# Cross-covariance attention on one core: stores two units later, and outputs of ten units laid out four heads wide

## The chip, the cores and the metric

The kernel runs on one core of a Trainium2 chip. The metric is the device time of one launch in microseconds (us). Engines are named as in the profile: PE is the matrix engine (PEld its weight loads), DVE the vector engine, ACT the scalar engine, POOL GpSimd, SP the engine whose queue issues every transfer here.

## The reference

```python
# Q, K, V: (8, 12, 512, 64) float32
Q_norm = Q / (np.linalg.norm(Q, axis=-2, keepdims=True) + 1e-10)
K_norm = K / (np.linalg.norm(K, axis=-2, keepdims=True) + 1e-10)
attn = np.einsum('bhnd,bhne->bhde', Q_norm, K_norm)          # 64 x 64 per head
attn = softmax(attn, axis=-1)
return np.einsum('bhnd,bhde->bhne', V, attn)                 # 512 x 64 per head
```

There are 96 heads. Three inputs and one output of 12.58 MB each have to cross between HBM and the core, 50.33 MB in all.

## The kernel before

**Units and pairs.** Four heads make a unit, so there are 24 units (u = 0 to 23). Q and K of a unit come as one 512 KB transfer each (`load_qk`, L72 and L73): partition 32h + i holds 16 successive rows of head h, 4 KB in one run. V comes for two units at once, a pair w = 0 to 11, as one 1 MB transfer (`load_v`, L77): each partition holds 32 successive rows, 8 KB in one run. The output of a unit goes out as one 512 KB transfer (`store`, L80), that of the last unit as two of 256 KB.

**One unit's way.** DVE casts Q and K to bfloat16, side by side (`cast_q` L84, `cast_k` L87). PE forms the Gram matrix of the joined 128 columns of each head (`grams`, 64 matmuls, L103): its diagonal gives both norms (`norms`, L115, L120), one off-diagonal block gives the logits. ACT saves that block (`keep_kq`), POOL scales it, PE transposes it (`logits`), DVE scales and ACT takes exponentials (`exps`, L139). `normalise` (L143 to L147) writes the softmax in bfloat16 into one of 12 buffers `ab`; `doubled` (L176, L177) copies it through PE and ACT to the other 64 partitions, so that `ab` holds a block diagonal of two copies and one matmul serves two rows of V.

**V and the outputs.** V of a pair is cast by ACT and DVE (`cast_v`, L96), transposed on PE eight 128x128 blocks at a time (`vtrans`, L155), and evicted by ACT into `vt` (L159). In `outs` (L179) the transposed V is the weight and `ab` the moving operand. An output bank `po` holds 128 partitions x 512 numbers: for two heads, x = 0 and 1, 64 columns of weights each (`MV = 64`), and four steps t. So a unit takes two banks of eight matmuls, each partition of a bank holds eight successive rows, and `store` writes runs of 2 KB:

```python
Of = out.rearrange("b h n d -> (b h n d)").rearrange("(u s p f) -> u p s f", s=SV, p=128, f=TP * 2 * D)
```

With A = 4 and TP = 4 a partition's 16 pieces of V are numbered (a, t).

**The order.** The program order of each engine is written out by hand. A main loop runs over steps s = 0 to 23: loads for unit s + 3, V loads, stores of the units up to `n1 - 3`, where `outs_by(s) = (s - 3) * 9 // 10` is the number of units whose outputs are computed by the end of step s; then the Gram part of unit s, logits of s - 1, normalisation of s - 2, outputs, and transposes of V. After step 23 a second loop computes the outputs of units 18 to 23 (i = 0 to 5): the Gram banks of PSUM are given over to a pool `ps_t` of four banks, in which `vtrans_f32` (L170, L171) transposes the last V uncast; `outs` there evicts one bank by ACT and one by DVE; `doubled(last)` stands at i = 3, ahead of the outputs of unit 21. The outputs use the two banks of `ps_o` throughout.

**Queues.** SP issues all 85 transfers in program order. Eight completion semaphores are handed out in turn, so each transfer waits until the one eight places before it has landed, and besides for its data or its buffer: a load of Q and K for the cast five units back (five buffers), a V load for the cast five pairs back, a store for its unit's evictions. An eviction of `outs` waits until the store ten units back has landed (ten buffers `so`).

Of the kernel before, what the change touches and what calls it, by code (L numbers as in the profile page):

```python
# [8 lines left out]
F32 = mybir.dt.float32  # L9
BF16 = mybir.dt.bfloat16  # L10
# [4 lines left out]
D = 64  # L15
HU = 4
# [1 line left out]
R = 16  # L18
HV = 8
NP = 16  # L20
A = 4
SV = 2
MV = 64
TP = 4


@with_exitstack
def kernel(
# [7 lines left out]
    nc = tc.nc  # L36
    B, H, N, _ = Q.shape
    assert N == NV * R and Q.shape[3] == D
    U = B * H // HU

    Qf, Kf = (x.rearrange("b h n d -> (b h n d)").rearrange("(u p f) -> u p f", p=128, f=R * D) for x in (Q, K))
    Vf = V.rearrange("b h n d -> (b h n d)").rearrange("(w p f) -> w p f", p=128, f=2 * R * D)
    Of = out.rearrange("b h n d -> (b h n d)").rearrange("(u s p f) -> u p s f", s=SV, p=128, f=TP * 2 * D)

    ctx.enter_context(tc.manual_schedule())

# [3 lines left out]
    vbp = ctx.enter_context(tc.tile_pool(name="vbp", bufs=3))  # L50
    qkp = ctx.enter_context(tc.tile_pool(name="qkp", bufs=4))
    vtp = ctx.enter_context(tc.tile_pool(name="vtp", bufs=3))
# [3 lines left out]
    ps_v = ctx.enter_context(tc.tile_pool(name="ps_v", bufs=1, space=bass.MemoryType.PSUM))  # L56
    ps_l = ctx.enter_context(tc.tile_pool(name="ps_l", bufs=1, space=bass.MemoryType.PSUM))
    ps_o = ctx.enter_context(tc.tile_pool(name="ps_o", bufs=2, space=bass.MemoryType.PSUM))
# [3 lines left out]
    def outs_by(s):  # L62

        return max(0, (s - 3) * 9 // 10)


    qf, kf, vf, vb, qkb, nsq, rq, kqs, sl, ex, vt, so, kq = ({} for _ in range(13))
# [7 lines left out]
    def load_v(w):  # L75
        vf[w] = vp.tile([128, 2 * R * D], F32, name="vf")
        nc.sync.dma_start(out=vf[w], in_=Vf[w])  # L77

    def store(u, g=slice(0, SV)):
        nc.sync.dma_start(out=Of[u][:, g], in_=so[u][:, g].rearrange("p s t d -> p s (t d)"))  # L80

    def cast_q(u):
        qkb[u] = qkp.tile([128, R, 2 * D], BF16, name="qkb")
# [5 lines left out]
    def cast_v(v):  # L89

        w, i = divmod(v, 2)
        if i == 0:
            vb[w] = vbp.tile([128, A, TP, 2 * D], BF16, name="vb")
        x = vf[w].rearrange("p (a t d) -> p a t d", a=A, d=2 * D)
        for t, copy in ((2 * i, nc.scalar.copy), (2 * i + 1, nc.vector.tensor_copy)):
            copy(vb[w][:, :, t], x[:, :, t])  # L96

    def grams(u):

# [29 lines left out]
    def logits(u):  # L129
        for h in range(HU):  # L130
            nc.tensor.transpose(lg[:, h, :], kqs[u][D:, h, :], ident[D:, D:])  # L131

    def scale_q(u):
        s = sl[u] = small.tile([D, HU, D], F32, name="sl")
        nc.vector.tensor_tensor(out=s, in0=lg, in1=rq[u][0:D, :, None].to_broadcast([D, HU, D]), op=ALU.mult)  # L135

    def exps(u):
        e = ex[u] = small.tile([D, HU, D], F32, name="ex")
        nc.scalar.activation(e, sl[u], AF.Exp)  # L139

    def normalise(u):
        s = small.tile([D, HU], F32, name="esum")
        nc.vector.reduce_sum(out=s, in_=ex[u], axis=AX.X)  # L143
        ri = small.tile([D, HU], F32, name="rinv")
        nc.vector.reciprocal(ri, s)
        a = abuf[u % len(abuf)]
        nc.vector.tensor_tensor(out=a[0:D, :, 0, :], in0=ex[u], in1=ri[:, :, None].to_broadcast([D, HU, D]), op=ALU.mult)  # L147

    def vtrans(v):

        w, i = divmod(v, 2)
        ps = ps_v.tile([128, A, 2, 128], BF16, name="vps")
        for t in range(2):
            for a in range(A):
                nc.tensor.transpose(ps[:, a, t, :], vb[w][:, a, 2 * i + t, :], identb)  # L155

        if i == 0:
            vt[w] = vtp.tile([128, TP, 128, A], BF16, name="vt")
        nc.scalar.copy(vt[w][:, 2 * i:2 * i + 2], ps.rearrange("p a t c -> p t c a"))  # L159

    def vtrans_f32(v):

        w, i = divmod(v, 2)
        if i == 0:
            vt[w] = vtp.tile([128, TP, 128, A], BF16, name="vt")
        for t in range(2 * i, 2 * i + 2):
            ps = ps_t.tile([128, 128, A], F32, name="vps32")
            for a in range(A):
                c = (a * TP + t) * 2 * D
                nc.tensor.transpose(ps[:, :, a], vf[w][:, c:c + 2 * D], ident)  # L170
            both[t % 2](vt[w][:, t], ps)  # L171

    def doubled(u):

        a = abuf[u % len(abuf)]
        nc.tensor.matmul(dup[D:], identb[0:D, 0:D], a[0:D, :, 0, :], tile_position=(0, D))  # L176
        nc.scalar.copy(a[D:, :, 1, :], dup[D:])  # L177

    def outs(u, copies=(nc.scalar.copy, nc.scalar.copy)):  # L179
        s = so[u] = sop.tile([128, SV, TP, 2 * D], F32, name="so")  # L180
        a = abuf[u % len(abuf)]
        v = vt[u // 2][:, :, u % 2 * 64:(u % 2 + 1) * 64]
        for g in range(SV):
            po = ps_o.tile([128, TP, 2 * D], F32, name="po")
            for t in range(TP):
                for x in range(2):
                    h = 2 * g + x
                    nc.tensor.matmul(  # L188
                        po[MV * x:MV * (x + 1), t, :], v[:, t, NP * h:NP * (h + 1), :].rearrange("p c a -> p (c a)"),
                        a[:, h].rearrange("p a d -> p (a d)"), tile_position=(0, MV * x),  # L190
                    )
            copies[g](s[:, g], po)  # L192

# [10 lines left out]
    ident = const.tile([128, 128], F32, name="ident")  # L204
    make_identity(nc, ident)
    identb = const.tile([128, 128], BF16, name="identb")
# [7 lines left out]
    def clear(i):  # L214

        nc.scalar.copy(abuf[i].rearrange("p h a d -> p (h a d)"), zeros)
# [4 lines left out]
    def on(f, u):  # L221
        if 0 <= u < U:
            f(u)
# [3 lines left out]
    nv, nst, nt = 0, 0, 0  # L227
    for s in range(U):
        n0, n1 = outs_by(s - 1), outs_by(s)
        on(load_qk, s + LOAD_AHEAD)  # L230
        while nv < (min(U, n1 + 7) // 2 if s >= 3 else 1):
            load_v(nv)
            nv += 1
        while nst < n1 - 3:
            store(nst)
            nst += 1
        new = range(nt, max(0, min(s - 2, n1 + 2)))
        if s > 4:
            for v in new:
                cast_v(v)  # L240
        on(cast_q, s + 1)
        on(normalise, s - 2)
        on(grams, s)
        on(norms, s)
        on(keep_kq, s)
        on(scale_k, s)
        on(logits, s - 1)
        on(scale_q, s - 1)
        on(exps, s - 1)
        on(cast_k, s + 1)  # L250
        if s <= 4:
            for v in new:
                cast_v(v)
        for v in range(n0, n1):
            outs(v)
        on(doubled, s - 2)
        if 6 <= s + 5 < len(abuf):
            clear(s + 5)
        for v in new:
            vtrans(v)  # L260
            nt = v + 1

    last = U - 1
    main.close()
    ps_t = ctx.enter_context(tc.tile_pool(name="ps_t", bufs=4, space=bass.MemoryType.PSUM))
    both = (nc.scalar.copy, nc.vector.tensor_copy)

    for i, u in enumerate(range(n1, U)):
        while nv < min(U, u + 8) // 2:
            load_v(nv)  # L270
            nv += 1
        store(u - 3)
        if i == 0:
            normalise(last - 1)
        if i == 2:
            scale_q(last)
            exps(last)
        if i == 3:
            normalise(last)
        on(vtrans_f32, u + 2)  # L280
        if i == 1:
            doubled(last - 1)
        if i == 3:
            doubled(last)
        outs(u, both)
        if i == 1:
            logits(last)
    for u in range(U - 3, last):
        store(u)
    for g in range(SV):  # L290
        store(last, slice(g, g + 1))
# [29 lines left out]
```

## Time and profile before

| | |
|---|---|
| median of 11 runs | 131.05 us (130.54 to 131.91) |
| profiled execution | 131.2 us, span 129.4 us |
| busy | PE 86.1, PEld 66.3, DVE 95.1, ACT 91.2, POOL 64.7 us |
| transfers | 15208 packets, 50.67 MB, mean 392 GB/s |
| Q, K, V and store issues | 24, 24, 12 and 25 |

The span runs from the first to the last of the program's own instructions; what lies around it makes up the other 1.8 us. The share of a transfer queue is the time its packets took, as a share of 16 transfer engines over the whole span. A line of the timeline gives start, duration, engine, line and operation, then in brackets how long the engine had been idle and what ended that. A matmul group's duration holds the latency of its last matmul.

### The profile page before, as it was taken

To read this page: it belongs to the slowest core of one execution; us is meant where nothing else is said; L and a number is where in the kernel's file an instruction comes from. 1 tells how busy PE (TensorE), PEld (TensorE's weight loads), DVE (VectorE), ACT (ScalarE), POOL (GpSimd) and SP (SyncE) were. 2 spreads that over 40 slices of the span, in tenths; PEclk is the share of its full clock that TensorE was granted. 3 is DMA by queue.
4 is the path that set the end of the run, shared out by engine and by line. 5 is a ranking of instruction groups with operands and counts; after the bars stand their busy time and mean duration, and the time that the engine had idled before them with its cause. 6 is when DMAs were issued, how large, how long until landed. Compare 5 with 4: busy or idle time off the path is not lost.

```text
span 129.4 us, 5390 instructions
## 1 busy us (share of the span) xinstructions
PE 86.1 (67%) x2232; PEld 66.3 (51%) x2232; DVE 95.1 (73%) x366; ACT 91.2 (70%) x171; POOL 64.7 (50%) x57
## 2 busy tenths in 40 slices
PE   0047565958856976849883697688486497859530
PEld 0046543837644854638652576465364385648420
DVE  0445979596998699894994968987993889648740
ACT  7601353675999999899596565999699398997520
POOL 4006775672698168656564761986267077500000
PEclk9999999999998599995999658999999859999955
DMA  4999999999999999999999999999999999999894
GB/s 139 348 386 427 414 408 410 423 408 406 418 405 420 403 409 419 411 404 432 399 412 419 411 411 413 429 406 408 422 411 406 421 419 405 403 389 362 321 340 163
DMA packets 15208, 50.67 MB, mean 392 GB/s; under 512 B 1360, under 2 KB 1360, under 8 KB 13648
## 3 DMA queue, kind: packets, MB, share of 16 engines
q1 hardware_dynamic: 15184, 50.34, 97.6%
q8 instruction: 17, 0.28, 0.9%
q14 instruction: 7, 0.06, 0.1%
HBM read 37.75 MB, written 12.58 MB: 389 GB/s over the span
## 4 chain that ended last, share of the span: by engine, by line
DMA 45%; DVE 15%; ACT 15%; PE 13%; issue 4%; SPq 3%; ACTq 0%; DVEq 0%
DMA qf<-in_Q_dram 28%; DMA out_dram<-so 9%; DMA vf<-in_V_dram 8%; PE gram L103 5%; DVE scr L115 5%; ACT so L192 4%; ACT vt L159 3%; PE po L188 3%; PE vps L155 3%; ACT ex L139 2%; DVE qkb L84 2%; ACT kq L108 2%; ACT vb L96 2%; PE vps L170 2%; DVE ab L147 1%
## 5 line engine op out<-in xcount | busy, mean ns | idle before, releaser
L120 POOL TENSOR_TENSOR rq<-nsq,mhalf 128x4 f32<-128x4 f32 x24 | 47.8, 1992 | 45.2 <-DVE nsq L115 28.9
L103 PE MATMUL gram<-qkb 32*128 32x128 bf16 x1536 | 35.8, 256 | 16.3 <-DVE qkb L87 10.6
L103 PEld LDWEIGHTS <-qkb 32*128 32x128 bf16 x1536 | 29.8, 115 | 22.6 <-DVE qkb L87 13.3
L115 DVE CUSTOM_DVE_ANT_0 scr<-gram,ident 128x128 f32<-128x128 f32 x96 | 22.0, 281 | 9.5 <-PE gram L103 9.5
L108 ACT COPY kq<-gram 64x256 f32<-64x256 f32 x24 | 8.8, 368 | 26.4 <-DVE nsq L115 26.2
L84 DVE CAST qkb<-qf 128x1024 bf16<-128x1024 f32 x24 | 16.6, 690 | 12.3 <-DMA qf<-in_Q_dram 12.3
L192 ACT COPY so<-po 128x512 f32<-128x512 f32 x42 | 22.8, 588 | 2.0 <-PE po L188 1.5
L188 PE MATMUL po<-ab,vt 128*64 128x128 bf16 x384 | 18.2, 232 | 5.4 <-ACT vt L159 2.9
L159 ACT COPY vt<-vps 128x1024 bf16<-128x1024 bf16 x20 | 20.2, 1012 | 0.7
L188 PEld LDWEIGHTS <-vt 128*64 128x64 bf16 x384 | 12.6, 115 | 9.6 <-ACT vt L159 4.1
L155 PEld LDWEIGHTS <-vb 128*128 128x128 bf16 x160 | 10.9, 110 | 12.8 <-ACT kq L108 6.3
L87 DVE CAST qkb<-kf 128x1024 bf16<-128x1024 f32 x24 | 16.2, 675 | 0.5 <-DMA kf<-in_K_dram 0.5
L125 POOL TENSOR_TENSOR kqs<-kq,rq 64x256 f32<-64x256 f32 x24 | 15.4, 641 | 1.9
L155 PE MATMUL vps<-identb,vb 128*128 128x128 bf16 x160 | 14.8, 247 | 1.6 <-ACT vb L96 1.6
L131 PE MATMUL lgdup<-ident,kqs 64*64 64x64 f32 x96 | 11.3, 247 | 5.1 <-POOL kqs L125 5.0
L176 PE MATMUL lgdup<-ab,identb 64*64 64x256 bf16 x24 | 7.3, 302 | 9.8 <-DVE sl L135 8.6
L96 ACT CAST vb<-vf 128x512 bf16<-128x512 f32 x20 | 12.4, 620 | 0.0
L131 PEld LDWEIGHTS lgdup<-ident,kqs 64*64 64x64 f32 x96 | 7.0, 122 | 9.1 <-POOL kqs L125 7.6
L139 ACT ACTIVATE ex<-sl 64x256 f32<-64x256 f32 x24 | 10.0, 417 | 1.4 <-DVE sl L135 0.6
L147 DVE TENSOR_TENSOR ab<-ex,rinv 64x256 bf16<-64x256 f32 x24 | 10.3, 427 | 0.8
L135 DVE TENSOR_TENSOR sl<-lgdup,rq 64x256 f32<-64x256 f32 x24 | 9.8, 410 | 1.0 <-PE lgdup L131 0.5
L143 DVE TENSOR_REDUCE esum<-ex 64x4 f32<-64x256 f32 x24 | 9.7, 403 | 1.2 <-ACT ex L139 1.1
(21 smaller groups left out, 58.1 us busy)
## 6 DMA issues: line engine op xcount, KB each, us to landing
qf<-in_Q_dram SPq DMA_DIRECT2D x24, 512.0 KB, 11.6
kf<-in_K_dram SPq DMA_DIRECT2D x24, 512.0 KB, 11.7
vf<-in_V_dram SPq DMA_DIRECT2D x12, 1024.0 KB, 13.0
out_dram<-so SPq DMA_DIRECT2D x23, 512.0 KB, 11.3
out_dram<-so SPq DMA_DIRECT2D x2, 256.0 KB, 3.2
```

The costliest lines, as they stand in the source:

```text
L84: nc.vector.tensor_copy(qkb[u][:, :, 0:D], qf[u])
L87: nc.vector.tensor_copy(qkb[u][:, :, D:], kf[u])
L96: copy(vb[w][:, :, t], x[:, :, t])
L103: nc.tensor.matmul(gbuf[:, h, 0:2 * D], x, x, start=(t == 0), stop=(t == R - 1), tile_position=(NV * h, 0))
L115: nc.vector.tensor_tensor_reduce(out=scr, in0=gbuf[:, h, 0:2 * D], in1=ident, scale=1.0, scalar=1e-20, op0=ALU.mult, op1=ALU.add, accum_ou ...
L120: nc.gpsimd.tensor_tensor(out=r, in0=n2, in1=mhalf, op=ALU.pow)
L125: nc.gpsimd.tensor_tensor(out=kk[D:], in0=kq[u][D:], in1=rq[u][D:, :, None].to_broadcast([D, HU, D]), op=ALU.mult,)
L131: nc.tensor.transpose(lg[:, h, :], kqs[u][D:, h, :], ident[D:, D:])
L155: nc.tensor.transpose(ps[:, a, t, :], vb[w][:, a, 2 * i + t, :], identb)
L159: nc.scalar.copy(vt[w][:, 2 * i:2 * i + 2], ps.rearrange("p a t c -> p t c a"))
L188: nc.tensor.matmul(po[MV * x:MV * (x + 1), t, :], v[:, t, NP * h:NP * (h + 1), :].rearrange("p c a -> p (c a)"), a[:, h].rearrange("p a d ...
L192: copies[g](s[:, g], po)
```

## The change

Three things are changed.

**Stores.** In the main loop `store` runs up to unit `n1 - 5` instead of `n1 - 3`, in the second loop it is `store(u - 5)` instead of `store(u - 3)`. The order of the stores among themselves stays; the loads behind them move ahead of two stores.

**The end.** `doubled(last)` stands at i = 4 instead of 3, behind the outputs of unit 21. The last two outputs (units 22, 23) take their banks from `ps_t`.

**Wide pairs.** For pairs 1, 4, 7, 10 and 11 (units 2, 3, 8, 9, 14, 15 and 20 to 23) a partition's pieces of V are numbered with A = 2 and T = 8. An output bank then holds all four heads with 32 columns of weights each (`MW = 32`) and four of eight steps t, so a bank takes 16 matmuls with weights of 128x32 in place of 8 with 128x64, and a partition holds 16 successive rows over the two banks: runs of 4 KB (the last unit goes out bank by bank, in runs of 2 KB). Casts, transposes and evictions keep their number and their size and read or write in another order.

```diff
+    Ow = out.rearrange("b h n d -> (b h n d)").rearrange("(u p f) -> u p f", p=128, f=TW * 2 * D)
+    wide = (1, 4, 7, 10, 11)
+
+    def parts(w):
+
+        return (2, TW) if w in wide else (4, TP)
...
     def store(u, g=slice(0, SV)):
-        nc.sync.dma_start(out=Of[u][:, g], in_=so[u][:, g].rearrange("p s t d -> p s (t d)"))
+        x = so[u][:, g].rearrange("p s t d -> p s (t d)")
+        o = Ow[u].rearrange("p (s f) -> p s f", s=SV) if u // 2 in wide else Of[u]
+        nc.sync.dma_start(out=o[:, g], in_=x)
...
-    def outs(u, copies=(nc.scalar.copy, nc.scalar.copy)):
+    def outs(u, copies=(nc.scalar.copy, nc.scalar.copy), bank=lambda: ps_o.tile([128, 512], F32, name="po")):
...
             for t in range(TP):
-                for x in range(2):
-                    h = 2 * g + x
+
+                for x, h in enumerate(range(HU) if w in wide else (2 * g, 2 * g + 1)):
+                    m = MW if w in wide else MV
+                    c = NP * (HU * j + h)
                     nc.tensor.matmul(
-                        po[MV * x:MV * (x + 1), t, :], v[:, t, NP * h:NP * (h + 1), :].rearrange("p c a -> p (c a)"),
-                        a[:, h].rearrange("p a d -> p (a d)"), tile_position=(0, MV * x),
+                        po[m * x:m * (x + 1), t, :],
+                        vt[w][:, g * TP + t if w in wide else t, c:c + NP, :].rearrange("p c a -> p (c a)"),
+                        a[:, h].rearrange("p a d -> p (a d)"), tile_position=(0, m * x),
                     )
...
-        while nst < n1 - 3:
+        while nst < n1 - 5:
             store(nst)
...
-        store(u - 3)
+        store(u - 5)
...
-        if i == 3:
+        if i == 4:
             doubled(last)
-        outs(u, both)
+        if i < 4:
+            outs(u, both)
+        else:
+            outs(u, both, bank_t)
...
-    for u in range(U - 3, last):
+    for u in range(U - 5, last):
         store(u)
```

More of the change, by code (lines that the diff above doesn't have):

```diff
@@ L20 @@
 NP = 16
-A = 4
 SV = 2
@@ L24 @@
 TP = 4
+MW = 32
+TW = 8
 @with_exitstack
@@ L91, in cast_v @@
         w, i = divmod(v, 2)
+        A, T = parts(w)
         if i == 0:
-            vb[w] = vbp.tile([128, A, TP, 2 * D], BF16, name="vb")
+            vb[w] = vbp.tile([128, 16, 2 * D], BF16, name="vb")
         x = vf[w].rearrange("p (a t d) -> p a t d", a=A, d=2 * D)
-        for t, copy in ((2 * i, nc.scalar.copy), (2 * i + 1, nc.vector.tensor_copy)):
-            copy(vb[w][:, :, t], x[:, :, t])
+        y = vb[w].rearrange("p (a t) d -> p a t d", a=A)
+        for q, copy in ((2 * i, nc.scalar.copy), (2 * i + 1, nc.vector.tensor_copy)):
+            t = slice(q * T // 4, (q + 1) * T // 4)
+            copy(y[:, :, t], x[:, :, t])
     def grams(u):
@@ L147, in normalise, with new_vt @@
         nc.vector.tensor_tensor(out=a[0:D, :, 0, :], in0=ex[u], in1=ri[:, :, None].to_broadcast([D, HU, D]), op=ALU.mult)
+    def new_vt(w):
+        A, T = parts(w)
+        vt[w] = vtp.tile([128, 16, 128], BF16, name="vt").rearrange("p x y -> p (x y)").rearrange("p (t c a) -> p t c a", t=T, a=A)
     def vtrans(v):
         w, i = divmod(v, 2)
-        ps = ps_v.tile([128, A, 2, 128], BF16, name="vps")
-        for t in range(2):
+        A, T = parts(w)
+        if i == 0:
+            new_vt(w)
+        ps = ps_v.tile([128, 8, 128], BF16, name="vps").rearrange("p (a t) c -> p a t c", a=A)
+        t0 = i * T // 2
+        for t in range(T // 2):
             for a in range(A):
[L155 to L159, printed above, removed]
+                nc.tensor.transpose(ps[:, a, t, :], vb[w][:, a * T + t0 + t, :], identb)
+        nc.scalar.copy(vt[w][:, t0:t0 + T // 2], ps.rearrange("p a t c -> p t c a"))
     def vtrans_f32(v):
         w, i = divmod(v, 2)
+        A, T = parts(w)
         if i == 0:
[L165 to L171, printed above, removed]
+            new_vt(w)
+        for q in range(2):
+            ps = bank_t().rearrange("p (t c a) -> p t c a", t=T // 4, a=A)
+            t0 = (2 * i + q) * T // 4
+            for t in range(T // 4):
+                for a in range(A):
+                    c = (a * T + t0 + t) * 2 * D
+                    nc.tensor.transpose(ps[:, t, :, a], vf[w][:, c:c + 2 * D], ident)
+            both[q](vt[w][:, t0:t0 + T // 4], ps)
     def doubled(u):
@@ L177, in doubled @@
         nc.scalar.copy(a[D:, :, 1, :], dup[D:])
-    def outs(u, copies=(nc.scalar.copy, nc.scalar.copy)):
+    def outs(u, copies=(nc.scalar.copy, nc.scalar.copy), bank=lambda: ps_o.tile([128, 512], F32, name="po")):
         s = so[u] = sop.tile([128, SV, TP, 2 * D], F32, name="so")
         a = abuf[u % len(abuf)]
-        v = vt[u // 2][:, :, u % 2 * 64:(u % 2 + 1) * 64]
+        w, j = divmod(u, 2)
         for g in range(SV):
-            po = ps_o.tile([128, TP, 2 * D], F32, name="po")
+            po = bank().rearrange("p (t d) -> p t d", t=TP)
             for t in range(TP):
-                for x in range(2):
-                    h = 2 * g + x
+                for x, h in enumerate(range(HU) if w in wide else (2 * g, 2 * g + 1)):
+                    m = MW if w in wide else MV
+                    c = NP * (HU * j + h)
                     nc.tensor.matmul(
-                        po[MV * x:MV * (x + 1), t, :], v[:, t, NP * h:NP * (h + 1), :].rearrange("p c a -> p (c a)"),
-                        a[:, h].rearrange("p a d -> p (a d)"), tile_position=(0, MV * x),
+                        po[m * x:m * (x + 1), t, :],
+                        vt[w][:, g * TP + t if w in wide else t, c:c + NP, :].rearrange("p c a -> p (c a)"),
+                        a[:, h].rearrange("p a d -> p (a d)"), tile_position=(0, m * x),
                     )
@@ L266, with bank_t @@
     both = (nc.scalar.copy, nc.vector.tensor_copy)
+    def bank_t():
+        return ps_t.tile([128, 512], F32, name="vps32")
     for i, u in enumerate(range(n1, U)):
```

## The prediction

> **What bounds the kernel now.** I read the slices first, then the queues, then stretches of the end.
>
> ```profile
> DMA  4999999999999999999999999999999999999894
> GB/s 139 348 386 427 414 408 410 423 408 406 418 405 420 403 409 419 411 404 432 399 412 419 411 411 413 429 406 408 422 411 406 421 419 405 403 389 362 321 340 163
> ...
> q1 hardware_dynamic: 15184, 50.34, 97.6%
> q8 instruction: 17, 0.28, 0.9%
> ```
>
> The transfer engines are full from the second slice to the 36th, at 400 to 430 GB/s; no compute engine is above 73% of the span. So the kernel is bound by its transfers, and what can be won is either fewer nanoseconds per byte or the bytes missing at the end. The stretches put numbers on the end (duration; PE, PEld, DVE, ACT, POOL busy; clock; transfer share; GB/s):
>
> ```profile
> 24.00:28.00 4.00, 2.54 (x68) 1.85 (x57) 2.54 (x13) 2.12 (x4) 1.95 (x3) 1.00 1.01 414
> ...
> 104.00:113.00 9.00, 7.91 (x206) 6.48 (x203) 7.05 (x32) 8.27 (x16) 6.10 (x6) 0.88 1.02 408
> 113.00:116.00 3.00, 1.39 (x23) 1.13 (x22) 1.55 (x3) 2.73 (x6) 0.00 (x0) 1.00 1.04 401
> 116.00:124.00 8.00, 6.36 (x105) 5.02 (x104) 5.94 (x12) 5.01 (x11) 0.00 (x0) 0.95 0.86 328
> ```
>
> From 116 to 124 us the engines are 86% busy: stores leave as fast as outputs are computed, about 2 us a unit, while a store needs 1.3 us (512 KB at 401 GB/s). The SP queue's waits say the same: the two that are not for an earlier transfer and are long belong to the stores.
>
> ```profile
> SPq L80 <- ACT ab L177: 8.4, 4, 3.8
> SPq L80 <- DVE so L192: 8.2, 5, 2.4
> ```
>
> Why outputs are late there is seen in the timeline. Loads still pace the last Gram steps (DVE stands idle for them), and at the very end PE waits for the doubling and for its two banks:
>
> ```profile
> 100.57 0.69 DVE L84 CAST qkb<-qf 128x1024 bf16<-128x1024 f32 x1 [2.30 <-DMA qf<-in_Q_dram]
> ...
> 104.89 0.69 DVE L84 CAST qkb<-qf 128x1024 bf16<-128x1024 f32 x1 [0.54 <-DMA qf<-in_Q_dram]
> ...
> 120.88 0.27 PE L176 MATMUL lgdup<-ab,identb 64*64 64x256 bf16 x1 [0.76 <-DVE ab L147]
> ...
> 121.07 0.64 PE L188 MATMUL po<-ab,vt 128*64 128x128 bf16 x16
> ...
> 122.21 0.70 PE L188 MATMUL po<-ab,vt 128*64 128x128 bf16 x16 [0.50 <-ACT so L192]
> ...
> 123.29 1.07 PE L188 MATMUL po<-ab,vt 128*64 128x128 bf16 x16 [0.39 <-ACT so L192]
> ...
> 124.40 0.69 DVE L192 COPY so<-po 128x512 f32<-128x512 f32 x1 [0.76 <-PE po L188]
> ```
>
> [...] its packet records average 85.3 ns for 2 KB (stores) and 163.3 ns for 4 KB (loads of Q, K), so two small ones cost 7.3 ns, or 4.5%, more; but that compares writes with reads. [...] a 16 KB instruction fetch at 118.4 us took 0.96 us of one engine, and the store landing next came 2.16 us after its predecessor, where 1.28 is usual. [...]
>
> **The change, part by part.** The sum is made against the profiled execution, 131.2 us (span 129.4), which lies 0.15 above the median.
>
> *Stores two places later.* No transfer is added. Past step 8 each load stands two stores earlier in SP's queue, so lands 2 x 1.26 = 2.5 us sooner (1.26 being 512 KB at 414 GB/s), and when V's last load has landed, 13 units of stores are left in place of 11. Their data wait is shorter, never longer. New waits: the loads now ask earlier for their buffers. The closest is Q of unit 14, issued at 49.2 us, then 46.7; its buffer's last cast ended at 45.9. The others have 1.9 us or more, and up to eight transfers, about 10 us, lie in the queue meanwhile: cost nothing. The eviction of unit 22 needs store 12, landed at 111.1, then about 113.5; it runs at 122: nothing. DVE waited for Q by 1.36, 0.90, 2.30 and 0.54 us at units 17, 20, 22, 23, 5.1 us that earlier loads can return, of which the 2.5 us of advance is the most that unit 23 can use.
>
> *What filling the end is worth.* From 116 to 124 the engines moved 2624 KB, which takes 6.54 us at 401 GB/s: 1.46 us missing. As landings count it, the last 11 units of stores took 14.85 us after V's last load (113.55 to 128.40), at the 1.28 of the full stretch 14.07: 0.78 missing. [...] I take 0.9, ends 0.5 and 1.46.
>
> *4 KB runs.* Nine units change (the tenth, the last, keeps 2 KB). From the stretches, 512 KB takes 1.307 us at 401 GB/s (2 KB stores alone) and 1.266 at 414 (large loads): 9 x 0.041 = 0.37. From the packet records 9 x 8 x 7.3 to 9.3 ns = 0.53 to 0.67, the longer if 4 KB is taken from the later loads (about 161 ns). If writes to HBM are limited by bytes, nothing[...]. I take 0.4, ends 0 and 0.7.
>
> *Wide outputs on PE.* Ten units get 32 matmuls for 16. The row of 0.64 us holds one latency of 0.22, so the spacing is 0.42/15 = 28 ns; the Gram matmuls reach 17 ns (64 in 1.30 us), and 0.64/16 = 40 ns is the plain quotient. With 28 ns a unit takes 0.22 + 31 x 0.028 = 1.09, +0.45 us; ends +0.11 (17 ns) and +0.82 (40 ns). PE lies partly on the chain of a step, behind ACT's eviction of V and ahead of the next Gram. Six wide units precede unit 23: 6 x 0.45 = 2.7 us against the returned 5.1, so unit 23's cast starts 2.4 us sooner instead of 2.5. The 160 extra pairs of instructions also mean about 1.2 more fetches of 16 KB, 1.05 us each on one engine of 16: under 0.1 in the mean. Casts, transposes and ACT's evictions (1012 ns) keep their sizes; I count other strides at nothing, with 0.1 us for each of ten ACT evictions as an upper end, which the same slack covers.
>
> *The end's order.* Outputs of 21 no longer stand behind the doubling, and 22 and 23 need not wait for evictions: 0.76 + 0.50 + 0.39, about 1.6 us less PE waiting. Four wide units there add 4 x 0.45 = 1.8. So the last eviction, now ending at 125.1, ends at 125.1 - 2.4 - 1.6 + 1.8 = 122.9. It is enough: the full queue would land the last store near 127.1, and 256 KB takes 3.2 us from issue to landing. So the end stays with the transfers, compute being 1 us early.
>
> Sum: -0.9 - 0.4 = -1.3 on 131.2, 129.9 for the profiled execution; 0.15 under that for a median, **129.8**.
>
> **The rivals.**
>
> *A, the forecast:* 129.8, its own range 128.8 to 130.4.
>
> *B, hidden anyway:* the last landing is set by one lagging engine, which never idled, and 2 KB writes cost the same per byte. For: the gap is 1.46 by the mean and 0.78 by landings, and the instruction fetch falls in just this stretch. Against: stores are issued at 117.9, 119.9 and 122.5 as soon as evicted, with two or three units ahead of them. Gain 0.1 to 0.5: 130.8.
>
> *C, PE becomes the bound:* four narrow tiles overlap less than I think. With e more per wide unit, the end of compute moves by the larger of -2.5 and -5.1 + 6e, then by 4e - 1.6. It is zero at e = 0.67, a spacing of 35 ns; at 40 ns (e = 0.82) it is +1.5 us and the stores end as just-in-time as now: 132.6. For: PE is 7.9 of 9 us busy from 104 to 113. Against: weight loads of half the columns should not take longer, and the Gram matmuls run at 17 ns with four tiles.
>
> *D, the change is not there:* 4 KB rows are cut in two on their way, and only the stores' order counts: 131.05 - 0.9, about 130.2.
>
> **How the numbers follow.** About 0.5% (0.65 us) is what a measurement of this kernel can tell from no change: faster means below 130.4, slower above 131.7. A has 0.55, B 0.20, C 0.16, D 0.09. A is nearly all faster (0.53), D by two thirds (0.06), B by a quarter (0.05): 0.64. C is slower but for a small part: 0.15. The rest, 0.21, is no change. The range leaves out half of C's tail and the largest gains: 128.7 to 132.2.
>
> **What would show it.** Right: in the profile after, no slice before the last below about 380 GB/s, the stretch 116 to 124 at a share of 1.0, fewer packets by 1152, SP's waits for ACT and DVE at L80's successor mostly gone, casts of units 17, 20 and 22 without waits for Q, the last eviction about 2 us sooner, 32 matmuls in about 1.1 us. B: the share is 1.0, yet the last landing has not moved. C: wide groups above 1.3 us, and stores still waiting for evictions. The prediction is wrong if the gaps stay, or if they go and the time is 131 all the same.

## The result, and the profile after

The change makes the kernel slower: 133.94 us (median of 12 runs, 132.85 to 135.01) against 131.34 for the kernel before (47 runs beside them); ratio 1.0186, 95% interval 1.0155 to 1.0217. The prediction was 129.8, faster, with 132.2 as its upper end. The ratio compares means without the runs in a slower state (135.01 is one), so it differs a little from the ratio of the medians. The profiled execution took 132.9 us, its span 130.8. It was the second fastest of the twelve (their median span is 131.9), so the two spans read below, 129.4 and 130.8, lie nearer to each other than the medians; what lies around the span also grew, from 1.8 us to 2.2 in the mean.

The same lines of the page as before, with the chain that ended last:

```profile
DMA  4999999999999999999999999999999999976775
GB/s 143 408 413 428 404 407 417 414 407 416 408 408 425 398 421 402 410 426 405 410 422 406 412 412 420 410 410 431 401 422 408 421 413 399 400 302 227 305 299 204
...
q1 hardware_dynamic: 14032, 50.34, 95.9%
q8 instruction: 18, 0.29, 0.9%
...
PE 30%; DVE 22%; ACT 18%; DMA 13%; issue 11%; DVEq 0%; SPq 0%; ACTq 0%
```

In the kernel before, the chain read (its page, the same part):

```profile
DMA 45%; DVE 15%; ACT 15%; PE 13%; issue 4%; SPq 3%; ACTq 0%; DVEq 0%
```

So the transfers no longer carry the chain; the compute engines do, PE first, and "issue", time in which an engine waited for nothing that the profile names, went from 4% to 11%. The gap at the end did not close but grew. The stretches of the kernel after (columns as before: duration; PE, PEld, DVE, ACT, POOL; clock; transfer share; GB/s):

```profile
104.00:113.00 9.00, 6.43 (x170) 5.06 (x169) 5.55 (x21) 6.91 (x14) 5.32 (x4) 0.81 1.02 405
113.00:116.00 3.00, 2.55 (x39) 1.98 (x37) 2.33 (x13) 2.38 (x6) 1.62 (x2) 1.00 0.84 331
116.00:124.00 8.00, 6.63 (x158) 5.22 (x155) 5.90 (x12) 6.58 (x14) 0.00 (x0) 1.00 0.72 275
```

From 116 to 124 us the share is 0.72, where it was 0.86. The loads did come earlier: in the trace's landings Q of unit 23 arrives at 101.5 us (before 104.9), V's last at 110.1 (before 113.5). But the Gram of unit 23 ends at 112.8 instead of 109.6, and the last eviction at 125.6 instead of 125.1. The engines had the data 3.4 us sooner and were later with the work.

Where PE loses it is in its own timeline of the kernel after, 91 to 107 us (the idle time before a group and what ended it stand in brackets):

```profile
90.99 0.95 PE L116 MATMUL gram<-qkb 32*128 32x128 bf16 x54
94.09 0.34 PE L116 MATMUL gram<-qkb 32*128 32x128 bf16 x10 [2.15 <-issue]
...
102.73 0.63 PE L212 MATMUL po<-ab,vt 128*32 128x128 bf16 x32
103.84 0.27 PE L198 MATMUL lgdup<-ab,identb 64*64 64x256 bf16 x1 [0.49 <-DVE sl L148]
104.04 0.51 PE L176 MATMUL vps<-identb,vb 128*128 128x128 bf16 x6
106.24 0.30 PE L176 MATMUL vps<-identb,vb 128*128 128x128 bf16 x2 [1.69 <-issue]
```

The kernel before has such a stop too:

```profile
98.14 1.01 PE L103 MATMUL gram<-qkb 32*128 32x128 bf16 x59
101.82 0.27 PE L103 MATMUL gram<-qkb 32*128 32x128 bf16 x5 [2.67 <-issue]
```

Two things are to be seen. In the kernel after PE stops in the middle of a run of like matmuls, 54 of 64 Grams done, 6 of 8 transposes done, where no operand can be missing, for 2.15 and 1.69 us. And 32 wide output matmuls take 0.63 us, as long as 16 narrow ones did (0.64). Some groups of both forms take longer (wide up to 1.05, narrow up to 1.33), but at its best the wide form itself is free.

**What the stops are.** I numbered PE's rows in the trace, 4813 in all: weight loads, matmuls and 29 semaphore and drain instructions alike. All eight stops of over 0.35 us stand ahead of rows 1473, 1985, 2497, 2753, 3265, 3521, 4033 and 4289: each is 193 plus a multiple of 256. Queue q8, "instruction", moved 18 packets of 16 KB; between 38.8 and 112.1 us there is one of them to every 256 rows, 64 bytes a row by that count. PE resumes 1.25 to 1.6 us after such a packet has ended: packets end at 56.12, 92.55 and 104.79 us, PE goes on at 57.41, 94.09 and 106.24. I read this as PE waiting for its next block of instructions, 256 of them in a packet. From 38.8 to 112.1 us PE begins a block every 6.11 us, thirteen boundaries spaced by 5.90 to 6.31: about 3.7 us from a block's begin to the start of the fetch packet, 1.04 us of packet, 1.4 us until PE goes on. The kernel before begins its blocks at 39.3 to 116.5 us with spacings of 5.1 to 7.9, five stops, 7.1 us in all; after there are eight, 11.7 us. By the page PE runs 2232 matmuls before and 2392 after, each with its weight load: 320 instructions more, 1.25 blocks, 7.6 us at 6.11. Of these 192, those of the six wide units 2, 3, 8, 9, 14 and 15, stand ahead of the last Gram, in the stretch where the transfers are full: 0.75 blocks, 4.6 us. PE's stops have grown by as much, from 7.1 us to 11.7.

### The profile page after: what moved, and what is told of

It reads as the page before. It is cut to its first block, busy times and chain, and to the rows that moved or that the text cites. A ratio compares the mean times of both kernels' runs of the same rounds, so it can differ in the third digit from the quotient of the medians.

```text
span 130.8 us, 5719 instructions
## 1 busy us (share of the span) xinstructions
PE 87.5 (67%) x2392; PEld 67.6 (52%) x2392; DVE 95.0 (73%) x366; ACT 91.1 (70%) x171; POOL 64.5 (49%) x57
## 4 chain that ended last, share of the span: by engine, by line
PE 30%; DVE 22%; ACT 18%; DMA 13%; issue 11%; DVEq 0%; SPq 0%; ACTq 0%
PE gram L116 15%; DMA qf<-in_Q_dram 10%; DVE scr L128 8%; PE vps L176 7%; ACT so L217 5%; ACT vt L178 4%; PE po L212 4%; DMA kf<-in_K_dram 3%; DVE sl L148 3%; ACT ex L152 3%; ACT vb L109 2%; PE lgdup L198 2%; ACT kq L121 2%; DVE qkb L94 2%; DVE qkb L97 2%
## 5 line engine op out<-in xcount | busy, mean ns | idle before, releaser
L116 PE MATMUL gram<-qkb 32*128 32x128 bf16 x1536 | 36.6, 259 | 18.8 <-DVE qkb L97 10.0
L116 PEld LDWEIGHTS <-qkb 32*128 32x128 bf16 x1536 | 30.5, 116 | 25.1 <-DVE qkb L97 12.6
L217 ACT COPY so<-po 128x512 f32<-128x512 f32 x40 | 21.7, 589 | 0.8 <-DMA out_dram<-so 0.2
L212 PE MATMUL po<-ab,vt 128*32 128x128 bf16 (+1 forms) x480 | 17.3, 241 | 4.2 <-ACT vt L178 1.7
L212 PEld LDWEIGHTS <-vt 128*32 128x32 bf16 (+1 forms) x544 | 13.0, 110 | 8.3 <-issue 4.7
L138 POOL TENSOR_TENSOR kqs<-kq,rq 64x256 f32<-64x256 f32 x24 | 14.9, 621 | 1.9
L144 PE MATMUL lgdup<-ident,kqs 64*64 64x64 f32 x96 | 11.8, 255 | 3.3 <-POOL kqs L138 2.3
```

Source lines behind the costliest of these rows:

```text
L116: nc.tensor.matmul(gbuf[:, h, 0:2 * D], x, x, start=(t == 0), stop=(t == R - 1), tile_position=(NV * h, 0))
L138: nc.gpsimd.tensor_tensor(out=kk[D:], in0=kq[u][D:], in1=rq[u][D:, :, None].to_broadcast([D, HU, D]), op=ALU.mult,)
L212: nc.tensor.matmul(po[m * x:m * (x + 1), t, :], vt[w][:, g * TP + t if w in wide else t, c:c + NP, :].rearrange("p c a -> p (c a)"), a[:, ...
```

## The experiments

**The theories.** F: PE's instructions are the bound; while the transfers are full, a block of 256 comes every 6.1 us, and the 320 more do the harm. W: the wide form costs time by its own work. S: the stores' new place does it. The counts of PE instructions in the expectations come from a listing that has 222 fewer; by the page they are 4464 for 4242 and 4784 for 4562, with the same differences. "Stops" are PE's idle times of over 0.35 us that end in "issue" after the first 35 us; they are read from one profiled execution of each kernel. All 63 stops of the table stand within two rows of 193 plus a multiple of 256. The kernel before was run beside each group of experiments: its median was 131.91 us beside e1 to e4, 131.33 beside e5, e6, e8 and e9, and 131.50 beside the others. So the ratios, not the times, are to be compared across the table.

| kernel | PE instructions | stops, us in all | time, us | ratio to before (95%) |
|---|---|---|---|---|
| before | 4464 | 5, 7.1 | | 1 |
| after | 4784 | 8, 11.7 | 133.94 | 1.0186 (1.0155 to 1.0217) |
| e1_narrow | 4464 | 6, 6.1 | 131.04 | 0.9964 (0.9940 to 0.9988) |
| e2_wide_alone | 4784 | 9, 12.0 | 134.96 | 1.0250 (1.0207 to 1.0293) |
| e3_split | 4784 | 9, 12.5 | 134.53 | 1.0217 (1.0166 to 1.0269) |
| e4_gram_pairs | 3248 | 1, 1.0 | 129.79 | 0.9876 (0.9827 to 0.9926) |
| e5_stores_alone | 4464 | 6, 8.5 | 131.31 | 1.0012 (0.9988 to 1.0035) |
| e6_end_alone | 4464 | 6, 6.2 | 131.45 | 0.9996 (0.9971 to 1.0021) |
| e8_before_gram_pairs | 2928 | 0, 0 | 131.18 | 0.9974 (0.9947 to 1.0002) |
| e7_wide_last | 4592 | not read | 131.34 | 0.9990 (0.9970 to 1.0010) |
| e7b_wide_first | 4656 | 7, 10.4 | 133.82 | 1.0167 (1.0121 to 1.0214) |
| e10_tall | 4208 | 3, 3.4 | 130.84 | 0.9966 (0.9945 to 0.9987) |
| e11_wide_tall | 4464 | 3, 3.7 | 131.48 | 1.0001 (0.9980 to 1.0021) |

**e1_narrow.** The kernel after without wide pairs.

```diff
-    wide = (1, 4, 7, 10, 11)
+    wide = ()
```

> The kernel after with no wide pairs: stores five units back and the end's order stay; PE has 4242 instructions again in place of 4562. Theory F (instruction supply: PE gets a block of 256 instructions, 16 KB, about every 6.1 us while the transfers are full, and the 320 more are 1.25 blocks): the loss goes, and the earlier loads and fuller end show: 129.8 to 131.0 us, three to five PE stalls of over 0.35 us at block ends as before, not eight. Theory W (the wide form costs time by its own work, on PE or in evictions): the same, 129.8 to 131.0, but the stalls not related. Theory S (the stores' new place does the harm, loads crowd out what the end needs): still 133 to 134.

131.04 us, 0.36% faster than before. The whole loss comes with the wide pairs, and S falls. There are six stops for the three to five that I expected. This run also tells against PE's busy time and its clock as the cause: in its profiled execution PE is busy for 92.6 us at a mean granted clock of 0.868, in that of the kernel after for 87.5 us at 0.893, and yet it is the faster one (131.53 us against 132.89).

**e2_wide_alone.** Wide pairs with the stores three units back and the end as before (`n1 - 3`, `store(u - 3)`, `doubled(last)` at i = 3, all outputs from `ps_o`).

> Wide pairs alone: the stores three units back and the end's order as in the kernel before. F: the supply limits PE as in the kernel after, seven to nine stalls, and loads cannot come earlier: 133 to 135 us. W: the same time, with the time lost in the steps of wide units only. S: 130.5 to 131.3[...].

134.96 us: wide pairs alone cost 2.5%; that this is more than with the other two edits is not resolved, since the intervals overlap.

**e3_split.** e1_narrow, with each output matmul of the ten units cut in two halves of 64 columns: narrow layout, 2 KB runs, but 320 instructions more.

```diff
+                    for k in ((0, 1), (1, 2)) if w in (1, 4, 7, 10, 11) else ((0, 2),):
-                    nc.tensor.matmul(po[m * x:m * (x + 1), t, :], ..., a[:, h]...)
+                        nc.tensor.matmul(po[m * x:m * (x + 1), t, D * k[0]:D * k[1]], ..., a[:, h, k[0]:k[1]]...)
```

> As e1_narrow (no wide pairs, runs of 2 KB, same casts, transposes and evictions), but each output matmul of the ten units that were wide is issued as two of 64 columns: PE has 4562 instructions, as the kernel after, at the same columns streamed. F: the loss is back, 132.5 to 134.5 us, with seven to nine stalls at multiples of 256 instructions. W: no loss, within 0.5 us of e1_narrow. S: as e1_narrow.

134.53 us. The loss is back without any wide output, with the same streamed columns; PE's busy time, 89.0 us, is below that of e1. PE's waits without a named releaser in this kernel (in total, times, longest):

```profile
PE gram L116 <- issue: 9.6, 7, 2.1
...
PE po L213 <- issue: 2.2, 2, 1.2
...
PE vps L176 <- issue: 0.9, 1, 0.9
```

They fall on whatever stands at the block's end: Grams, outputs, a transpose. W cannot explain this run; F can.

**e4_gram_pairs.** The kernel after, with Gram matmuls that stream two row groups at once (the odd rows of Q and K are left out of the Gram matrix): as many columns, half the instructions.

```diff
-        for t in range(R):
+        for t in range(0, R, 2):
...
-                nc.tensor.matmul(gbuf[:, h, 0:2 * D], x, x, ...)
+                nc.tensor.matmul(gbuf[:, h, 0:4 * D], x, y, ...)     # y: rows t and t + 1, 256 columns
```

> The kernel after with 32 Gram matmuls of 256 columns a unit in place of 64 of 128: as many columns streamed, 1536 PE instructions fewer (3026). It leaves out the odd rows of Q and K from the Gram matrix; all else runs as in the kernel after. F: PE's stalls go, compute keeps up with the loads, the stretch 116 to 124 us of the transfers is full: 128 to 130 us. W: no change, 133 to 134, since wide outputs are all there. S: 133 to 134.

129.79 us, with all ten units wide. The stretches of this kernel at the end, and below them the last one of e8_before_gram_pairs:

```profile
113.00:116.00 3.00, 3.00 (x48) 2.34 (x50) 2.20 (x5) 2.04 (x6) 0.00 (x0) 1.00 1.03 410
116.00:124.00 8.00, 3.60 (x137) 2.68 (x129) 4.64 (x9) 3.60 (x8) 0.00 (x0) 0.88 1.02 397
...
116.00:124.00 8.00, 5.98 (x102) 4.62 (x101) 6.12 (x12) 5.09 (x11) 0.00 (x0) 1.00 0.82 312
```

PE's busy time over the span is 85.1 us, only 2.4 below the kernel after, so it is hardly its work that was taken away. The transfers are now full to the end, as the prediction had drawn it.

**e8_before_gram_pairs.** The same edit in the kernel before.

> The kernel before with 32 Gram matmuls of 256 columns a unit in place of 64 of 128 (the odd rows of Q and K are left out of the Gram matrix): 1536 PE instructions fewer, the same columns. It tells what the change brings where PE's instructions are no limit, by comparison with e4_gram_pairs (129.8). F: the kernel before is held by the same supply, less: 130.3 to 131.0, no PE stalls; e4 is then faster by 0.5 to 1.3, which is what the earlier loads and the 4 KB runs are worth. If the before has no loss to PE's instructions: 131.2 to 131.9.

131.18 us, no stop at all. The interval of its ratio reaches to 1.0002: that the kernel before lost anything to its five stops is not resolved. Against this one, e4 is faster by 0.9876/0.9974, about 1.0% or 1.3 us (the intervals of the two ratios reach 0.5% and 0.3% to either side, together about 0.7 us): this is what the change is worth where PE's instructions do not limit.

**e5_stores_alone** and **e6_end_alone.** The stores' edit alone in the kernel before; the end's edit alone in the kernel before.

> The kernel before with the stores five units back in both loops and nothing else. F (PE is fed 256 instructions per about 6.1 us while transfers are full, so earlier loads find PE unable to use them): casts no longer wait for Q, PE stalls at block ends instead, 130.8 to 131.6 us, no change. S (the stores' new place alone is worth the 0.9 us that the prediction gave it): 130.0 to 130.6.

> The kernel before with the end's order alone: last doubling behind the outputs of unit 21, last two outputs in the banks of V's transposes; stores three units back, no wide pairs. F: the last eviction comes 1 to 1.5 us sooner, but the stores still wait for outputs before: 130.5 to 131.3. If the end's order is all of the gain of e1_narrow: 130.7 to 131.0, as that one.

131.31 and 131.45 us: neither moves the time by itself. With earlier loads alone (e5) the casts of units 17, 20 and 23 do not wait for Q and that of unit 22 waits 1.00 us, but PE's stops add up to 8.5 us instead of 7.1. e6 loads as late as before. Its last eviction came 0.5 us sooner, not the 1 to 1.5 that I expected, and its time lies above my range. The two together (e1) give 0.36%; that it takes both is not resolved, as the intervals of e1 and e6 overlap.

**e7_wide_last** and **e7b_wide_first.** The kernel after with `wide = (10, 11)` and with `wide = (1, 4, 7)`.

> The kernel after with only the last two pairs (units 20 to 23) wide: 128 PE instructions more than e1_narrow, all behind the last Gram, where no PE stall was seen. F (supply of PE's instructions): as e1_narrow, 130.7 to 131.4 us. If each wide unit costs time by itself (2.9 us over ten): 1.2 us more than e1_narrow, 131.9 to 132.5.

> The kernel after with pairs 1, 4 and 7 wide alone: 192 PE instructions more than e1_narrow, all in the stretch where the transfers are full. F: three quarters of a block more, 132.3 to 133.6 us, most of the loss. If each wide unit costs the same: six tenths of it, 132.5 to 133.0, and e7_wide_last has the rest.

131.34 and 133.82 us. (The profiled execution of e7_wide_last took 212.5 us, so its trace is not read.) Four wide units behind the last Gram cost little, 0.3% against e1, which the intervals do not resolve. Six in the full stretch cost 2%, nearly the whole loss, and more than the 133.6 us that F allowed: their 192 instructions are all of the 320 that stand ahead of the last Gram. A fixed cost for each wide unit would have put e7 at 131.9 or more and e7b at 133.0 or less.

**e11_wide_tall.** The kernel after with Q and K of units 7, 8, 13, 15 and 20 loaded so that a head lies on 64 partitions, in two runs of 2 KB; the Gram of such a unit takes 32 matmuls over 64 rows for 64 over 32. This gives back the 320 instructions, in five of the steps in which wide outputs are computed. Ahead of the last Gram PE then has 128 fewer than in the kernel before.

```diff
+            for t in range(R // 2):
+                for h in range(HU):
+                    x = qkb[u][D * (h % 2):D * (h % 2 + 1), h // 2 * (R // 2) + t, :]
+                    nc.tensor.matmul(gbuf[:, h, 0:2 * D], x, x, ..., tile_position=(D * (h % 2), 0))
```

> The kernel after, all ten units wide, with Q and K of units 7, 8, 13, 15 and 20 laid out two heads at a time as in e10_tall: PE has 4242 instructions, as before, and the full result. F: the loss is gone, 130.4 to 131.4 us. If wide outputs cost by themselves: 133.5 to 134.5.

131.48 us with all ten units wide, 0.1 above what F allowed: the loss is gone, though PE is as busy as in the kernel after (87.3 us against 87.5). Its Grams stream half the columns for these units, so it is e3 and e4, not this run, that tell the count of instructions from the columns.

**e10_tall.** e1_narrow with four such units (7, 11, 15, 19), 256 instructions below the kernel before.

> e1_narrow with Q and K of units 7, 11, 15 and 19 laid out two heads at a time (64 partitions a head, two runs of 2 KB a partition): 32 Gram matmuls over 64 rows in place of 64 over 32, 256 PE instructions fewer (3986), and eight transfers of 512 KB in runs of 2 KB. The result is the full one. F: one block less, stalls fall to two or three, minus 0.3 to 1 us of the time, plus 8 x 0.04 to 0.08 us for the shorter runs: 130.2 to 131.0 us. Without F: e1_narrow plus 0.3 to 0.6.

130.84 us, 0.9966: faster than before, and not to be told from e1. Three stops of 3.4 us remain and the end is full (share 0.98 from 116 to 124 us), but eight loads now go in 2 KB runs. These two, e1 and e10, are faster than both the kernel before and the kernel after.

**e9_light.** The kernel after with less to move: K of units 5 to 23 is that of the first five, outputs of units 0 to 15 are not stored.

```diff
+            kf[u] = kf[u % 5]        # u >= 5, no load
...
+        if u < 16:
+            return                   # in store
```

> The kernel after, its PE instructions untouched, with fewer bytes: K of units 5 to 23 is not loaded (the first five units' K is used again) and outputs of units 0 to 15 are not stored. F[...]: from block end to the next fetch's start clearly less than the 2.9 to 4 us of the kernel after, blocks possible in under 5 us, no stall over 0.35 us or one or two. Against it, a fetch that takes its 6 us whatever the load: again seven or eight stalls, spaced by 6 us.

One run, 125.7 us. The page of this kernel:

```profile
DMA  3999999999999888594466698489300000447593
...
q1 hardware_dynamic: 7712, 31.98, 67.9%
```

Three stops, 3.4 us in all, between what F (none to two) and a fetch of fixed length (seven or eight) had led me to expect. Between 38 and 106 us a fetch packet starts 1.2 us after the block's begin (median; 3.7 in the kernel after), and blocks begin every 4.4 to 6.7 us. Within this one trace the wait goes with the load. Of the thirteen blocks, the seven in which the transfer engines were nearly idle between begin and fetch (a share of 0.13 or less) waited 0.1 to 1.2 us, the six with a share of 0.65 to 1.01 waited 2.5 to 4.5 us. So the fetch is slow in good part because the transfer engines are busy; whether the wait is spent in a queue or before the fetch is asked for, the trace does not tell.

## Why the prediction was wrong

- **Stores two places later:** right for the transfers. Q of unit 23 came 3.4 us sooner; 0.4 was there by unit 11 already, before the stores' place can tell, and in e5, with this edit alone, it came 2.7 us sooner. Casts of units 17, 20, 22, 23 no longer waited, and no load waited longer for its buffer (0.4 us at the most, before 0.6).
- **4 KB runs and filling the end:** the sum of -1.3 us agrees with e4 against e8, about -1.3, where PE's instructions do not limit. The mechanism of forecast A exists: the end is full there (share 1.02 against 0.82). That the sizes agree so closely is luck, with 0.7 us of uncertainty, and how much is filling and how much the longer runs was not told apart. In the kernel after it was covered by another limit: SP's waits for the doubling at a store, which were to go, grew from 8.4 us to 10.2.
- **Wide outputs on PE, the step that failed.** It was costed in streaming time: +0.45 us a unit at a spacing of 28 ns. Measured: nothing, 0.63 us for 32 matmuls against 0.64 for 16, a spacing of some 13 ns by the prediction's own reckoning (an estimate: 0.63 less 0.22, over 31). The weight loads of 128x32 took 104 ns each in the mean, those of 128x64 in the same trace 119. The same step named the 1.2 more instruction fetches and put them at under 0.1 us, as time of the transfer engines. That term was mis-sized: as time that PE needs to be given its instructions, the 192 that stand ahead of the last Gram are 0.75 x 6.11 = 4.6 us, and PE's stops grew by 4.6 us, from 7.1 to 11.7. The other 128 came behind it and cost little (e7).
- **The slack** of 5.1 us was not there to be used. It was counted from DVE's waits for Q, but with Q early the same steps wait for PE's instructions: thirteen block boundaries in a row at 6.11 us. In the kernel before the eleven blocks from 39.25 to 108.57 us took 6.30 us each, so against 6.11 they had only some 2.1 us to spare, an estimate. 4.6 us against that is a loss of about 2.5; the last Gram ended 3.1 us later.
- **The end's order:** from the last Gram to the last eviction 12.9 us, before 15.4, and in e6, with this edit alone, 12.9 too. So this edit did what was said, but e6 as a whole was no faster; in its profiled execution the last Gram came 2.0 us later than before.
- **Rival C** named the right engine and sign and put its time at 132.6, but by a price, the spacing of matmuls, that was not the one. Its evidence, PE 7.9 of 9 us busy, pointed at busy time; the sign that mattered was PE's idle time marked "issue". It stood in the kernel before as well, 2.67 us in the middle of a Gram at 101.8 us, in a line that the prediction did not read.

## What to carry to other kernels

Look at the waits of PE that end in "issue", in the middle of a run of like matmuls: in this kernel they recurred every 256 instructions, and the count of instructions was the cost of an edit on PE, not the columns it streams (e3 against e1: 320 more at the same columns, 134.53 us for 131.04; e4 against the kernel after: 1536 fewer at the same columns, 129.79 us for 133.94). A block cost 6.1 us while the transfers were full, 24 ns an instruction (6.11 over 256), so a form that doubled the matmuls to save an estimated 0.4 us of transfers lost (e2, 2.5%). The slack of an engine that waits for loads is worth only what the next limit leaves of it: take the loads away on paper and ask what would be waited for then.

## What the runs showed of the hardware

- Output matmuls with weights of 128x32 in four tiles took, at their best, half as long each as those of 128x64 in two: 32 in 0.63 us, 16 in 0.64.
- PE's instructions came in blocks of 256 by packets of 16 KB on their own queue; with the transfer engines full (a share of 1.02 from 104 to 113 us), one every 6.11 us, with 1.4 us from the packet's end to the next instruction. Over these twelve blocks PE went no faster than that, though its busy share was only 67% of the span.
- With less to move (e9) blocks came in as little as 4.4 us. After the last Gram, with the transfers at a share of 0.72, one block of the kernel after was through in 3.5 us (from 120.9 to 124.4); its successor's packet started 0.2 us after its begin instead of 3.7. Why it came so early there is not shown.
